# Ada columns loaded one pair ahead and pinned on VectorE, and spread otherwise over a two-layer decoder trunk

## Chip, cores, metric

The kernel runs on one core of one Trainium2 chip. The time is device microseconds for one execution of the whole program. It is compared as the median of several runs.

## What is computed

A trunk of two layers, 256 tokens of 1024 numbers. Layer 0 mixes tokens with a gated convolution, layer 1 with differential attention; a product-key expert layer ("peer", 16384 experts) follows each mixer. Each of these four sub-layers is modulated by a vector c:

```python
def ada_mod(c, w, b):
    m = silu(c) @ w + b            # w: 1024 x 3072
    shift, scale, gate = split(m, 3)
    return shift, 1.0 + scale, 1.0 + gate
for i in range(2):
    shift, scale, gate = ada_mod(c, ada_w[i, 0], ada_b[i, 0])
    f = (short_conv_mixer if i == 0 else diff_attention)(x * scale + shift, ...)
    x = layer_norm(alpha * x + gate * f, ln_g[i, 0], ln_b[i, 0])
    shift, scale, gate = ada_mod(c, ada_w[i, 1], ada_b[i, 1])
    f = peer_ffn(x * scale + shift, w_q, sub_keys, u, v)   # u, v: 16384 x 1024 each
    x = layer_norm(alpha * x + gate * f, ln_g[i, 1], ln_b[i, 1])
```

## The kernel before

**Matrix products.** TensorE (PE) works in a format with a shortened mantissa, so each fp32 operand is split in a high and a low part and each product is made of three. A weight block of 128x1024 fp32 (512 KB) goes through `load`: SyncE (SP) issues its DMA into a buffer `raw`; ScalarE (ACT) copies the high part (L87); VectorE (DVE) subtracts it for the low part (L90, below "subtraction"). The two parts take two of the ten `spt` buffers, so five blocks can be split at once. `raw` has six buffers; the conv mixer adds twelve of its own and attention four. SP issues in a fixed order, and a DMA waits on SP until the last reader of its buffer is done: for a weight block that is its subtraction.

**Ada products.** One pair is two columns of 128x1024 of `ada_w`: `ada_column` loads a column into a `raw` buffer, and one DVE instruction multiplies it by silu(c) and adds it up (L177, "product"). Four pairs make a unit, which ends in one small addition (L186). Twelve pairs run in the conv mixer, 24 in peer 0 and four in peer 1, from generators called `fill`, one pair at each `advance(fill)`; `drain` runs the rest.

**The peer layer.** `steps()` yields steps which `pipeline(steps, 3)` runs: the first half of a step (loads and splits) is issued three steps ahead of its second half (matmuls). Below a V step is one block of `peer_v`: 12 matmuls of 128x512. Two V steps share one `wh` (ACT copy of the gated activations, L87) and one `wl` (its DVE subtraction, L90), each with two buffers. The order is U steps; U with gates; a stretch with U, V and gates; V with gates; and last a stretch of 40 V steps, called the last V stretch here and numbered from 0. Gates are DVE instructions (L824 to L828, L839) around small matmuls (L837). In the last V stretch X, the layer's input, is also multiplied by `ln_g` and has `ln_b` added: `Norm.affine`, four DVE instructions of 128x1024 (L297), behind two loads into `raw` buffers. The matmul loop is the same for all.

**The conv mixer** ends with y (L375 to L378, DVE), from which the output projection's matmuls (L351) follow.

**What sets the order.** A scheduler orders the instructions of each engine when the kernel is built, unless `keep_in_program_order` pins one behind all that was traced on its engine before it. In the conv mixer SP's DMAs are pinned so (`ordered` isn't empty). How often the fill advances:

```python
                if n % 2 == 1:               # U, V and gates
                    yield advance(fill)
...
                if n % 3 == 2:               # the last V stretch
                    yield advance(fill)
```

Of the kernel before, what the change touches and what calls it, by code (L numbers as in the profile page):

```python
# [11 lines left out]
F32 = mybir.dt.float32  # L12
# [8 lines left out]
P = 128  # L21
T = 256
NT = T // P
# [20 lines left out]
def tile_trunk(ctx: ExitStack, tc: tile.TileContext, x, c, columns, ada_w, ln_g, ln_b, conv_w_in_a, conv_w_in_b,  # L44
# [134 lines left out]
    def ada_unit(i, s, part):  # L179
        a = small.tile([P, KC], F32, tag="ada", name="ada", bufs=2)  # L180
        for q in range(KC // 2):
            for f in [ada_column(i, s, part, n, a[:, n:n + 1]) for n in (2 * q, 2 * q + 1)]:
                f()
            yield
        at = slice(None), 2 * i + s, slice(KC * part, KC * part + KC)
        dve.tensor_tensor(mod[at], a, ada_bT[at], op=ALU.add)  # L186
        yield
# [47 lines left out]
    class Norm:  # L235
# [56 lines left out]
        def affine(self, _):  # L292

            gb = ln_params(self.i, self.s)
            for t in range(NT):
                for n, op in enumerate((ALU.mult, ALU.add)):
                    dve.tensor_tensor(X[:, t, :], X[:, t, :], gb[n], op=op)  # L297
# [158 lines left out]
    def attn_mixer(j, li, hT, ap, prep, late):  # L456
# [145 lines left out]
        def steps():  # L602
# [10 lines left out]
            for h0 in range(0, HEADS, 2):  # L613
# [14 lines left out]
                if h0 == 4:  # L628
                    yield None, late
# [15 lines left out]
    def peer(i, hT, pp, fill, prep, late):  # L645
# [239 lines left out]
        def steps():  # L885
# [29 lines left out]
            for n, (gs, u) in enumerate(zip(gates(1, n2), us(2))):  # L915
                yield next(v01)
                yield u
                yield from gs
                if n % 2 == 1:
                    yield advance(fill)  # L920
# [5 lines left out]
            for n, v in enumerate(vs(2)):  # L926
                yield v
                if n % 3 == 2:
                    yield advance(fill)
                if n == 6:  # L930
                    yield None, late
                if n == n2 - 8:
                    yield drain(fill)
                    yield None, prep
# [5 lines left out]
    def units(*which):  # L940
        for w in which:
            yield from ada_unit(*w)

    with tc.tile_pool(name="cp", bufs=1) as cp, tc.tile_pool(name="cs", bufs=12) as more:
        streams.append(more)
        hT = [ht.tile([P, KC, T], F32R, tag=n, name=n) for n in ("hh", "hl")]
        fill = units((0, 0, 2), (0, 1, 0), (0, 1, 1))
# [5 lines left out]
    fill = units((0, 1, 2), (1, 0, 0), (1, 0, 1), (1, 0, 2), (1, 1, 0), (1, 1, 1))  # L953
    with tc.tile_pool(name="pp", bufs=1) as pp:
        late, norm = norm.affine, Norm(0, 1, (1, 0), ada)
        acc = peer(0, hT, pp, fill, norm.prepare, late)
    hT = norm(acc)
    with tc.tile_pool(name="ap", bufs=1) as ap, tc.tile_pool(name="as", bufs=4) as more:
        streams.append(more)
        late, norm = norm.affine, Norm(1, 0, (1, 1), ada)  # L960
# [3 lines left out]
    with tc.tile_pool(name="pp", bufs=1) as pp:  # L964
        late, norm = norm.affine, Norm(1, 1, None, ada)
        acc = peer(1, hT, pp, units((1, 1, 2)), norm.prepare, late)
# [49 lines left out]
```

## Time and profile before

| | |
|---|---|
| median of 3 runs | 1965.9 us (1965.88 to 1968.01) |
| profiled execution | 1965.55 us |
| its span, first to last instruction | 1963.8 us |
| mean granted TensorE clock | 0.985 |
| busy: PE, DVE, ACT | 1888.5, 1554.3, 899.7 us |
| chain of work that ended last | PE 91%, DVE 4%, DMA 3% |

A profile is of one execution. Its timelines give start and length of each instruction or run of like ones, and in brackets how long the engine was idle before and what released it. Idle time of PE is what counts first here.

### The profile page before, as it was taken

Reading aid. Unit: us, or ns where it says so; the run is one execution under the profiler, and the core shown is the slowest. Engines: PE = TensorE matmul, PEld = TensorE weight load, DVE = VectorE, ACT = ScalarE, POOL = GpSimd, SP = SyncE. Lnnn points to the kernel's source line nnn. Section 1 sums busy time; section 2 is a strip of 40 time slices with the busy share of each in tenths; the row PEclk is TensorE's granted clock in tenths of the full one; section 3 lists DMA queues with packets and bytes.
Section 4 is the critical chain, followed back from the end, with each engine's and each line's share of the span. In section 5 each row is a group of like instructions: output and inputs, shape, how many; then the busy total and the mean of one; then the engine's idle time right before and its main releaser. Section 6 shows DMA issues by size and latency. Waiting matters only on the chain.

```text
span 1963.8 us, 36953 instructions
## 1 busy us (share of the span) xinstructions
PE 1888.5 (96%) x14858; PEld 1722.1 (88%) x14858; DVE 1554.3 (79%) x3150; ACT 899.7 (46%) x1179; POOL 9.5 (0%) x28
## 2 busy tenths in 40 slices
PE   7959999999999999989989899999999999999997
PEld 6949999999999988877789699999999999888786
DVE  7988987887888888876677789878877766788755
ACT  4524555434444444434465545554344444444443
POOL 0000000000000000000100000000000000000000
PEclk9979999999999999989999899999999999999999
DMA  9954556556777765557754245555567555555563
GB/s 384 370 172 151 174 174 188 158 162 211 243 241 257 236 204 172 172 181 265 260 171 138 76 151 177 178 183 161 162 209 225 176 175 173 172 172 176 173 195 100
DMA packets 104412, 378.87 MB, mean 193 GB/s; under 512 B 11568, under 2 KB 12208, under 8 KB 104240
## 3 DMA queue, kind: packets, MB, share of 16 engines
q1 hardware_dynamic: 104096, 376.42, 59.4%
q8 instruction: 116, 1.90, 0.4%
q14 instruction: 56, 0.46, 0.1%
q10 hardware_dynamic: 144, 0.09, 0.0%
HBM read 375.42 MB, written 1.05 MB: 192 GB/s over the span
## 4 chain that ended last, share of the span: by engine, by line
PE 91%; DVE 4%; DMA 3%; issue 1%; ACT 1%; SPq 0%; DVEq 0%; ACTq 0%
PE acc L873 34%; PE ps L141 15%; PE ps L142 15%; PE ps L143 15%; PE ps L837 4%; PE acc L351 2%; PE acc L142 2%; PE acc L141 1%; PE acc L143 1%; DVE spt L90 1%; DVE raw L177 1%; DMA raw<-in_ada_w 1%; DMA raw<-in_conv_w_in_a 1%; DMA X<-in_x 1%; PE ps L516 0%
## 5 line engine op out<-in xcount | busy, mean ns | idle before, releaser
L87 ACT ACTIVATE spt<-raw 128x1024 fp32r<-128x1024 f32 x608 | 640.6, 1057 | 737.7 <-PE ps L142 415.6
L90 DVE TENSOR_TENSOR spt<-raw,spt 128x1024 fp32r<-128x1024 f32 x608 | 739.8, 1220 | 161.9 <-ACT spt L87 157.4
L141 PE MATMUL ps<-hh,spt 128*128 128x256 f32 x2400 | 685.4, 286 | 3.5 <-DVE hh L214 3.5
L142 PE MATMUL ps<-hl,spt 128*128 128x256 f32 x2400 | 681.2, 284 | 0.2
L143 PE MATMUL ps<-hh,spt 128*128 128x256 f32 x2400 | 680.6, 284 | 0.0
L873 PE MATMUL acc<-spt,wh 128*128 128x512 f32 x2048 | 567.0, 396 | 3.5 <-ACT wh L87 3.5
L141 PEld LDWEIGHTS ps<-hh,spt 128*128 128x128 f32 x2400 | 460.8, 192 | 7.3 <-issue 4.2
L142 PEld LDWEIGHTS ps<-hl,spt 128*128 128x128 f32 x2400 | 461.4, 192 | 3.9 <-DVE hl L90 0.7
L143 PEld LDWEIGHTS ps<-hh,spt 128*128 128x128 f32 x2400 | 461.3, 192 | 0.0
L873 PEld LDWEIGHTS acc<-spt,wh 128*128 128x128 f32 x2048 | 376.8, 189 | 75.5 <-ACT wh L87 3.8
L873 PE MATMUL acc<-spt,wl 128*128 128x512 f32 x1024 | 320.1, 392 | 5.6 <-DVE wl L90 5.6
L873 PEld LDWEIGHTS acc<-spt,wl 128*128 128x128 f32 x1024 | 191.9, 188 | 47.2 <-DVE wl L90 7.6
L177 DVE SCALAR_TENSOR_TENSOR raw<-raw,csb 128x1024 f32<-128x1024 f32 x96 | 116.2, 1220 | 55.7 <-DMA raw<-in_ada_w 55.5
L839 DVE SCALAR_TENSOR_TENSOR ring<-ps,ring 128x368 f32<-128x368 f32 (+2 forms) x192 | 98.1, 511 | 70.1 <-PE ps L837 69.4
L87 ACT ACTIVATE wh<-ring 128x512 fp32r<-128x512 f32 x128 | 79.9, 627 | 159.4 <-PE acc L873 149.7
L824 DVE TENSOR_TENSOR A<-iota_e,jT 128x1024 f16<-128x1024 f16 x192 | 130.7, 682 | 0.0
L828 DVE TENSOR_TENSOR B<-B,gT 128x368 f16<-128x368 f16 (+2 forms) x384 | 124.4, 332 | 3.9
L90 DVE TENSOR_TENSOR wl<-ring,wh 128x512 fp32r<-128x512 f32 x128 | 87.9, 688 | 38.8 <-ACT wh L87 38.4
L837 PEld LDWEIGHTS <-A 128*128 128x128 f16 x3072 | 91.0, 96 | 31.2 <-issue 14.7
L837 PE MATMUL ps<-B,A 128*128 128x46 f16 (+2 forms) x3072 | 111.9, 182 | 6.7 <-DVE B L828 6.7
L804 ACT ACTIVATE ring<-ps 128x512 f32<-128x512 f32 x128 | 74.6, 583 | 33.8 <-PE ps L143 33.8
L826 DVE TENSOR_TENSOR B<-iota_e,iT 128x368 f16<-128x368 f16 (+2 forms) x192 | 63.1, 330 | 0.0
(203 smaller groups left out, 1175.9 us busy)
## 6 DMA issues: line engine op xcount, KB each, us to landing
raw<-in_peer_u SPq DMA_DIRECT2D x256, 512.0 KB, 3.9
raw<-in_peer_v SPq DMA_DIRECT2D x256, 512.0 KB, 3.9
raw<-in_ada_w SPq DMA_DIRECT2D x96, 512.0 KB, 4.7
raw<-in_peer_w_q SPq DMA_DIRECT2D x32, 512.0 KB, 3.9
raw<-in_attn_w_qk SPq DMA_DIRECT2D x16, 512.0 KB, 4.3
raw<-in_conv_w_in_a SPq DMA_DIRECT2D x12, 512.0 KB, 10.2
raw<-in_conv_w_in_b SPq DMA_DIRECT2D x12, 512.0 KB, 10.2
raw<-in_conv_w_out SPq DMA_DIRECT2D x8, 512.0 KB, 6.9
```

What stands on the lines that cost most here:

```text
L87: act.activation(o, i, AF.Copy, scale=scale)
L90: return eng.tensor_tensor(o, a, b, op=ALU.subtract)
L141: pe.matmul(ps, ah, bh, start=first, stop=False)
L142: pe.matmul(ps, ah, bl, start=False, stop=False)
L143: pe.matmul(ps, al, bh, start=False, stop=last)
L177: return lambda: dve.scalar_tensor_tensor(w, w, 1.0, csb, op0=ALU.mult, op1=ALU.mult, accum_out=dst)
L804: act.activation(ring[:, s:s + 2, :].rearrange("p j t -> p (j t)"), st["ps"], AF.Gelu)
L824: dve.tensor_tensor(by_two(A), numbers(0, KEYS), pairs(jT, KEYS), op=ALU.is_equal)
L828: dve.tensor_tensor(by_two(B[:, h]), by_two(B[:, 1]), pairs(gT[:, h], n), op=ALU.mult)
L837: pe.matmul(ps[:, t, :], A[:, t, :], B[:, h, t, :], start=h == 0, stop=h == 1)
L839: dve.scalar_tensor_tensor(r, ps.rearrange("p t j -> p j t"), 1.0 / GSCALE, r, op0=ALU.mult, op1=ALU.mult)
L873: pe.matmul(acc[t][hf], lhs[:, jj, rows], rhs[:, hf * 512:(hf + 1) * 512], start=first and jp == 0 and jj == 0, stop=last and last_pair an ...
```

## The change

The generator of ada products now loads a pair's two columns one advance before it multiplies them, and outside the conv mixer pins the products where they are traced on DVE. The affine becomes a step with a first half (the two loads, so three steps ahead) and a second (the four DVE instructions, pinned). The fill advances on every third step instead of every second in the stretch with U, V and gates, and on every second instead of every third in the last V stretch, up to step 29. So peer 0 makes 13 of its 24 pairs ahead of the last V stretch's own advances instead of 16, and 11 instead of 8 there.

```diff
-    def ada_unit(i, s, part):
-        a = small.tile([P, KC], F32, tag="ada", name="ada", bufs=2)
-        for q in range(KC // 2):
-            for f in [ada_column(i, s, part, n, a[:, n:n + 1]) for n in (2 * q, 2 * q + 1)]:
-                f()
-            yield
-        at = slice(None), 2 * i + s, slice(KC * part, KC * part + KC)
-        dve.tensor_tensor(mod[at], a, ada_bT[at], op=ALU.add)
-        yield
+    def ada_units(*which):
+
+        def compute(at, a, fs, final):
+            for f in fs:
+                ins = f()
+                if not ordered:
+                    tc.keep_in_program_order(ins)
+            if final:
+                dve.tensor_tensor(mod[at], a, ada_bT[at], op=ALU.add)
+
+        loaded = None
+        for i, s, part in which:
+            a = small.tile([P, KC], F32, tag="ada", name="ada", bufs=3)
+            at = slice(None), 2 * i + s, slice(KC * part, KC * part + KC)
+            for q in range(KC // 2):
+                fs = [ada_column(i, s, part, n, a[:, n:n + 1]) for n in (2 * q, 2 * q + 1)]
+                if loaded:
+                    compute(*loaded)
+                    yield
+                loaded = at, a, fs, q == KC // 2 - 1
+        compute(*loaded)
         yield
...
-        def affine(self, _):
-
-            gb = ln_params(self.i, self.s)
-            for t in range(NT):
-                for n, op in enumerate((ALU.mult, ALU.add)):
-                    dve.tensor_tensor(X[:, t, :], X[:, t, :], gb[n], op=op)
+        def affine(self):
+
+            def first():
+                return ln_params(self.i, self.s)
+
+            def second(gb):
+                for t in range(NT):
+                    for n, op in enumerate((ALU.mult, ALU.add)):
+                        tc.keep_in_program_order(dve.tensor_tensor(X[:, t, :], X[:, t, :], gb[n], op=op))
+
+            return first, second
...
-                if n % 2 == 1:
+                if n % 3 == 2:
                     yield advance(fill)
...
-                if n % 3 == 2:
+                if n % 2 == 1 and n < n2 - 10:
                     yield advance(fill)
                 if n == 6:
-                    yield None, late
+                    yield late
```

The first place is the last V stretch of peer 0 on DVE. Each `wl` waits for PE to have done with the pair of steps two before it, so it tells how far DVE is ahead of PE. Before, around one pair of columns there (the first `wl` is that of steps 12 and 13, the second that of 14 and 15):

```order
1101 L90 TENSOR_TENSOR wl<-ring,wh 128x512 [waits PE_49,Activation_49]
1102 L90 TENSOR_TENSOR spt<-raw,spt 128x1024 [waits DMAHW3_49,Activation_49]
1103 L90 TENSOR_TENSOR spt<-raw,spt 128x1024 [waits DMAHW6_49,PE_49,Activation_49]
1104 L90 TENSOR_TENSOR wl<-ring,wh 128x512 [waits PE_49,Activation_49]
1105 L90 TENSOR_TENSOR spt<-raw,spt 128x1024 [waits DMAHW7_49,Activation_49]
1106 L177 SCALAR_TENSOR_TENSOR raw,ada<-raw,csb 128x1024 [waits DMAHW4_49,DVE_49]
1107 L90 TENSOR_TENSOR spt<-raw,spt 128x1024 [waits DMAHW0_49,PE_49,Activation_49]
1108 L177 SCALAR_TENSOR_TENSOR raw,ada<-raw,csb 128x1024 [waits DMAHW5_49,DVE_49]
1109 L90 TENSOR_TENSOR wl<-ring,wh 128x512 [waits PE_49,Activation_49]
```

And now, from the `wl` of steps 12 and 13 on; five such rows, here called a period, stand there seven times in all:

```order
1100 L90 TENSOR_TENSOR wl<-ring,wh 128x512 [waits PE_49,Activation_49]
1101 L90 TENSOR_TENSOR spt<-raw,spt 128x1024 [waits DMAHW6_49,Activation_49]
1102 L90 TENSOR_TENSOR spt<-raw,spt 128x1024 [waits DMAHW7_49,Activation_49]
1103 L177 SCALAR_TENSOR_TENSOR raw,ada<-raw,csb 128x1024 [waits DMAHW4_49]
1104 L177 SCALAR_TENSOR_TENSOR raw,ada<-raw,csb 128x1024 [waits DMAHW5_49]
1105 L90 TENSOR_TENSOR wl<-ring,wh 128x512 [waits PE_49,Activation_49]
1106 L90 TENSOR_TENSOR spt<-raw,spt 128x1024 [waits DMAHW2_49,Activation_49]
1107 L90 TENSOR_TENSOR spt<-raw,spt 128x1024 [waits DMAHW3_49,Activation_49]
1108 L177 SCALAR_TENSOR_TENSOR raw,ada<-raw,csb 128x1024 [waits DMAHW0_49,DVE_49]
1109 L177 SCALAR_TENSOR_TENSOR raw,ada<-raw,csb 128x1024 [waits DMAHW1_49,DVE_49]
```

What moved: before, DVE subtracted blocks 16 and 17 behind the `wl` of steps 14 and 15; now it subtracts blocks 11 and 12 behind the `wl` of steps 12 and 13. So against the same `wl` it does blocks of three steps less. The wait for PE at every second subtraction (its `spt` buffer, just coming free) is gone, and both products of a pair stand behind both subtractions.

On SP, in the same stretch, before:

```order
137 L69 DMA raw<-in_ada_w 128x1024 x2
138 L69 DMA raw<-in_peer_v 128x1024 x3
139 L69 DMA raw<-in_ada_w 128x1024 x2
140 L69 DMA raw<-in_peer_v 128x1024 x3
141 L69 DMA raw<-in_ada_w 128x1024 x2
142 L69 DMA raw<-in_peer_v 128x1024 x3
143 L69 DMA raw<-in_ada_w 128x1024 x2
```

And now:

```order
138 L69 DMA raw<-in_ada_w 128x1024 x2
139 L69 DMA raw<-in_peer_v 128x1024 x2
140 L69 DMA raw<-in_ada_w 128x1024 x2
141 L69 DMA raw<-in_peer_v 128x1024 x2
142 L69 DMA raw<-in_ada_w 128x1024 x2
143 L69 DMA raw<-in_peer_v 128x1024 x2
144 L69 DMA raw<-in_ada_w 128x1024 x2
145 L69 DMA raw<-in_peer_v 128x1024 x2
146 L69 DMA raw<-in_ada_w 128x1024 x2
```

What moved: two loads of ada columns now stand behind every two loads of V, not every three or six. The two V loads of a period take the two `raw` buffers of the two V blocks just ahead of them, from here to the end of the fill; the other four buffers hold two pairs of columns.

The second place is the way into that stretch on DVE, with the last gates and X's affine, before:

```order
1070 L828 TENSOR_TENSOR B<-B,gT 128x320 [waits DVE_49]
1071 L90 TENSOR_TENSOR spt<-raw,spt 128x1024 [waits DMAHW0_49,PE_49,Activation_49]
1072 L828 TENSOR_TENSOR B<-B,gT 128x320 [waits DVE_49] x2
1073 L177 SCALAR_TENSOR_TENSOR raw,ada<-raw,csb 128x1024 [waits DMAHW7_49]
1074 L828 TENSOR_TENSOR B<-B,gT 128x320 [waits DVE_49]
1075 L839 SCALAR_TENSOR_TENSOR ring<-ps,ring 128x40x8 [waits PE_49]
1076 L177 SCALAR_TENSOR_TENSOR raw,ada<-raw,csb 128x1024 [waits DMAHW0_49]
1077 L839 SCALAR_TENSOR_TENSOR ring<-ps,ring 128x40x8 [waits PE_49]
1078 L90 TENSOR_TENSOR wl<-ring,wh 128x512 [waits Activation_49] x2
1079 L297 TENSOR_TENSOR X<-X,raw 128x1024 [waits DMAHW3_49]
1080 L297 TENSOR_TENSOR X<-X,raw 128x1024
1081 L90 TENSOR_TENSOR spt<-raw,spt 128x1024 [waits DMAHW1_49,PE_49,Activation_49]
```

And now, from the `wl` of steps 8 and 9 on (ahead of it stand, in this order, the `wl` of the first two pairs of steps, the subtraction of block 5, `wl`, the subtraction of 6, two products, `wl`, the subtraction of 7 and two products):

```order
1088 L90 TENSOR_TENSOR wl<-ring,wh 128x512 [waits PE_49,Activation_49]
1089 L187 TENSOR_TENSOR mod<-ada,smT 128x8 [waits DVE_49]
1090 L90 TENSOR_TENSOR spt<-raw,spt 128x1024 [waits DMAHW1_49,Activation_49]
1091 L90 TENSOR_TENSOR spt<-raw,spt 128x1024 [waits DMAHW2_49,Activation_49]
1092 L313 TENSOR_TENSOR X<-X,raw 128x1024 [waits DMAHW4_49]
1093 L90 TENSOR_TENSOR wl<-ring,wh 128x512 [waits PE_49,Activation_49]
1094 L313 TENSOR_TENSOR X<-X,raw 128x1024 [waits DMAHW5_49,DVE_49]
1095 L313 TENSOR_TENSOR X<-X,raw 128x1024
1096 L90 TENSOR_TENSOR spt<-raw,spt 128x1024 [waits DMAHW3_49,Activation_49]
1097 L177 SCALAR_TENSOR_TENSOR raw,ada<-raw,csb 128x1024 [waits DMAHW7_49]
1098 L177 SCALAR_TENSOR_TENSOR raw,ada<-raw,csb 128x1024 [waits DMAHW0_49]
1099 L313 TENSOR_TENSOR X<-X,raw 128x1024 [waits DVE_49]
```

What moved: before, a product stood among the last gates' B's and another between the two L839, each of a column loaded just before. Now both stand together ahead of the last three B's, and the two products that stood one gate group earlier have gone. Behind the gates, three pairs of products stand among the subtractions of blocks 6 to 10, and X's affine (L313 now), which stood ahead of block 5, stands behind block 9.

## Rows read from the trace of the kernel before

**Rows 1.** The page: groups (busy, mean ns, idle before), then a DMA median to landing.
```profile
L87 ACT ACTIVATE spt<-raw 128x1024 fp32r<-128x1024 f32 x608 | 640.6, 1057 | 737.7 <-PE ps L142 415.6
L90 DVE TENSOR_TENSOR spt<-raw,spt 128x1024 fp32r<-128x1024 f32 x608 | 739.8, 1220 | 161.9 <-ACT spt L87 157.4
...
L177 DVE SCALAR_TENSOR_TENSOR raw<-raw,csb 128x1024 f32<-128x1024 f32 x96 | 116.2, 1220 | 55.7 <-DMA raw<-in_ada_w 55.5
...
raw<-in_peer_v SPq DMA_DIRECT2D x256, 512.0 KB, 3.9
```

**Rows 2.** Busy time by stretch, columns in its first line.
```profile
core 0: us, PE busy (x) PEld busy (x) DVE busy (x) ACT busy (x) POOL busy (x), PEclk, DMA share, GB/s
...
100.00:120.00 20.00, 8.05 (x35) 6.22 (x33) 20.00 (x39) 1.25 (x2) 0.00 (x0) 0.77 0.79 261
480.00:700.00 220.00, 220.00 (x1790) 200.71 (x1787) 184.73 (x306) 96.50 (x111) 0.00 (x0) 1.00 0.75 245
840.00:866.00 26.00, 19.59 (x167) 15.71 (x166) 20.77 (x39) 8.91 (x11) 0.00 (x0) 0.85 0.66 214
866.00:886.00 20.00, 20.00 (x76) 16.08 (x76) 10.19 (x11) 7.74 (x10) 0.00 (x0) 0.85 0.53 158
```

**Rows 3.** Timeline of PE, end of peer 0; idle and releaser in brackets.
```profile
858.80 0.22 PE L837 MATMUL ps<-B,A 128*128 128x40 f16 x1 [2.78 <-DVE B L828]
860.17 0.21 PE L837 MATMUL ps<-B,A 128*128 128x40 f16 x1 [1.16 <-DVE B L828]
...
865.81 3.78 PE L873 MATMUL acc<-spt,wh 128*128 128x512 f32 x8 [2.20 <-ACT wh L87]
```

**Rows 4.** Waits: engine, line, released by: us in total, times, longest.
```profile
DVE raw L177 <- DMA raw<-in_ada_w: 55.5, 31, 4.3
...
PE acc L873 <- DVE wl L90: 5.6, 4, 1.9
```

**Rows 5.** Timeline of DVE over the same stretch.
```profile
853.67 1.23 DVE L177 SCALAR_TENSOR_TENSOR raw<-raw,csb 128x1024 f32<-128x1024 f32 x1 [1.06 <-DMA raw<-in_ada_w]
...
861.43 1.23 DVE L177 SCALAR_TENSOR_TENSOR raw<-raw,csb 128x1024 f32<-128x1024 f32 x1 [1.08 <-DMA raw<-in_ada_w]
...
885.63 1.23 DVE L177 SCALAR_TENSOR_TENSOR raw<-raw,csb 128x1024 f32<-128x1024 f32 x1 [3.83 <-DMA raw<-in_ada_w]
...
886.78 0.69 DVE L90 TENSOR_TENSOR wl<-ring,wh 128x512 fp32r<-128x512 f32 x1
```

**Rows 6.** Chain of waits, 840 to 990 us: start, length, what.
```profile
839.92 2.72 PE acc L873 x12
...
859.91 3.47 DMA raw<-in_ada_w
...
873.06 4.67 DMA raw<-in_peer_v
...
880.70 4.84 DMA raw<-in_ada_w
```

**Rows 7.** Timeline of ACT in the last V stretch.
```profile
915.90 0.63 ACT L87 ACTIVATE wh<-ring 128x512 fp32r<-128x512 f32 x1 [1.66 <-PE acc L873]
...
918.62 1.06 ACT L87 ACTIVATE spt<-raw 128x1024 fp32r<-128x1024 f32 x1 [1.14 <-PE acc L873]
```

**Rows 8.** Timeline of DVE, end of the conv mixer.
```profile
85.78 1.23 DVE L90 TENSOR_TENSOR spt<-raw,spt 128x1024 fp32r<-128x1024 f32 x1 [0.81 <-ACT spt L87]
...
89.57 1.23 DVE L90 TENSOR_TENSOR spt<-raw,spt 128x1024 fp32r<-128x1024 f32 x1 [1.69 <-ACT spt L87]
...
119.36 0.75 DVE L378 TENSOR_TENSOR y<-y,g 128x256 f32<-128x256 f32 x2
```

**Rows 9.** Timeline of PE, same place.
```profile
120.28 3.78 PE L351 MATMUL acc<-spt,yh 128*128 128x512 f32 x8 [12.23 <-ACT yh L87]
```

**Rows 10.** Timeline of PE, peer 1, entry to the last V stretch.
```profile
1842.78 2.10 PE L873 MATMUL acc<-spt,wh 128*128 128x512 f32 x8 [1.32 <-ACT wh L87]
1845.96 1.19 PE L873 MATMUL acc<-spt,wl 128*128 128x512 f32 x4 [1.08 <-DVE wl L90]
```

More of the change, by code (lines that the diff above doesn't have):

```diff
@@ L927, in steps @@
                 yield v
-                if n % 3 == 2:
+                if n % 2 == 1 and n < n2 - 10:
                     yield advance(fill)
                 if n == 6:
-                    yield None, late
+                    yield late
                 if n == n2 - 8:
@@ L937, in peer @@
         return acc
-    def units(*which):
-        for w in which:
-            yield from ada_unit(*w)
     with tc.tile_pool(name="cp", bufs=1) as cp, tc.tile_pool(name="cs", bufs=12) as more:
@@ L946, in tile_trunk @@
         hT = [ht.tile([P, KC, T], F32R, tag=n, name=n) for n in ("hh", "hl")]
-        fill = units((0, 0, 2), (0, 1, 0), (0, 1, 1))
+        fill = ada_units((0, 0, 2), (0, 1, 0), (0, 1, 1))
         norm = Norm(0, 0, (0, 1), cp)
@@ L952, in tile_trunk @@
     ordered.clear()
-    fill = units((0, 1, 2), (1, 0, 0), (1, 0, 1), (1, 0, 2), (1, 1, 0), (1, 1, 1))
+    fill = ada_units((0, 1, 2), (1, 0, 0), (1, 0, 1), (1, 0, 2), (1, 1, 0), (1, 1, 1))
     with tc.tile_pool(name="pp", bufs=1) as pp:
-        late, norm = norm.affine, Norm(0, 1, (1, 0), ada)
+        late, norm = norm.affine(), Norm(0, 1, (1, 0), ada)
         acc = peer(0, hT, pp, fill, norm.prepare, late)
@@ L959, in tile_trunk @@
         streams.append(more)
-        late, norm = norm.affine, Norm(1, 0, (1, 1), ada)
+        late, norm = norm.affine(), Norm(1, 0, (1, 1), ada)
         acc = attn_mixer(0, 1, hT, ap, norm.prepare, late)
@@ L964, in tile_trunk @@
     with tc.tile_pool(name="pp", bufs=1) as pp:
-        late, norm = norm.affine, Norm(1, 1, None, ada)
-        acc = peer(1, hT, pp, units((1, 1, 2)), norm.prepare, late)
+        late, norm = norm.affine(), Norm(1, 1, None, ada)
+        acc = peer(1, hT, pp, ada_units((1, 1, 2)), norm.prepare, late)
     norm(acc)
```

## Prediction

> **What bounds the kernel now.** First the page's table: PE is busy 1888.5 of 1963.8 us, so about 75 us of PE idle time are all that a change of VectorE and DMA order can touch, and much of it belongs to the start and the norms. Then the busy time by stretch [rows 2]: in the long stretch with U, V and gates (480 to 700 us) PE is busy 220.00 of 220 us although pairs of products run there; nothing is to be had there. At the end of the conv mixer it is the reverse: DVE is busy 20.00 of 20 us, PE 8.05. In the last stretches of peer 0 both have gaps. Then the waits [rows 4]: DVE waits 55.5 us for columns of `ada_w`, in 31 places. That is much, but idle time of DVE; PE waits for a `wl` in four places, 5.6 us in all. So the time the change aims at is mostly time in which PE worked on. What PE does wait for in its last V stretch shows on its timeline [rows 3] and in the chain [rows 6]: a few us. On ACT, a high part is copied there as soon as PE frees a buffer ("1.14 <-PE acc") [rows 7]: before, weights are as far ahead as the five pairs of `spt` buffers allow. That lead is what hides DVE's waits.
>
> **Peer 0's last V stretch, the main term.** A V step takes PE 2.72 us [rows 6], two take 5.44. DVE's work for two steps is now one `wl`, two subtractions and two products. On the timeline the product at 885.63 and the `wl` at 886.78 start 1.15 apart, and the next instruction 0.60 behind the `wl` [rows 5]; a subtraction is as long as a product (mean 1220 ns both) [rows 1]. So 0.60 + 4 x 1.15 = 5.2 us of 5.44: it fits, barely.
>
> What doesn't fit is the way through the two `raw` buffers left for V. The load of block k+2 is issued when block k's subtraction ends. It lands, ACT copies 1.06 us [rows 1], DVE subtracts (1.2 us with its start), and the hand-overs take some 0.05 each. So a buffer goes round once in the landing time plus 2.3 us, and PE wants it each 5.44: the landing would have to take 3.1 us or less. No row has that. The shortest load on the chain took 3.47, the median of V is 3.9, a V load behind another 4.67, and the first column of a pair 4.84 [rows 1, 6]. The first load of a period is issued 2.2 us behind the last column, the second 1.2 us behind the first. I take 4.1 us for the first (just over the median) and 4.7 for one right behind another (the 4.67 row). So a period takes 4.1 + 2.3 = 6.4 us, 1.0 longer than PE's.
>
> Now block by block, in us from PE's start of step 0 (step k would end at 2.72 (k+1)); five blocks are ready at 0, as before. Block 5 is subtracted by 5.0, as PE frees its buffer at 2.7. Then `wl` waits for the end of step 1 and block 6 is done at 8.4; products to 10.7. Block 7's load was issued at 9.5, behind the affine's two: landed 14.2, copied 15.3, done 16.4; in time (wanted at 19.0), but it holds DVE up, and two products follow to 18.7. Block 8's buffer came free with the first of them at 17.55: landed 22.25, done 24.5, wanted at 21.8: **PE waits 2.7.** Block 9 is done at 25.7; three of the affine's instructions and a `wl` follow to 29.7. Block 10, issued at 24.5: done 30.9, wanted 29.9: **1.0.** Products, the affine's last and `wl` to 34.9. Block 11, issued at 30.9: landed 35.0, done 37.3, wanted 33.6: **3.7.** From here the periods run as above, and blocks 13, 15, 17, 19, 21 and 23 are late by 1.0 each: **6.0.** Sum 13.4 us. Against it stand the waits for `wl` of before, which the new order replaces: 5.6 less the 1.08 that is peer 1's [rows 4, 10], 4.5. Term: **+8.9.** With 3.5 us for every landing the same walk gives about 6 (block 8 0.3, block 10 0.4, block 11 3.1, the rest 0.4 each), so +1.5; with 4.84 for all about 19 (2.9, 1.7, 4.4, and 1.7 each), so +14.5. Those are its bounds.
>
> The page "DMA: Bandwidth & Descriptors" of the Trainium skill (Anatomy of one DMA, the GpSimd path) gives a fixed 2.0 us plus bytes over 436 GB/s. By it, as an estimate, a block of 512 KB would land in 3.2 us and the period would be 5.5 us, so that the steady part would cost next to nothing. The trace disagrees: 3.47 is the shortest here, for a load that had nothing right ahead of it, and the median is 3.9 [rows 1, 6].
>
> **The last gates of peer 0.** PE idles 2.78 + 1.16 + 2.20 us between 856 and 865.8 [rows 3], since B's stand behind products, and products behind columns just loaded (1.06 and 1.08 us of waits on DVE) [rows 5]. Without the earlier pair (two products and the 1.06: 3.4 us) the first of the last B's is ready at 857.1. A subtraction and two products, which need not wait any more, follow to 860.5, three B's to 861.2, the gate matmuls to 861.9; ring and `wh` (0.4 and 0.63 [rows 7]) and hand-overs bring step 0 to 863.2. The other rings also wait on PE, whose clock is at half there (below), so I take 863.9 and not 865.81: **-1.9** (bounds -0.9 and -2.6).
>
> **Conv mixer.** The matmuls at 120.28 waited 12.23 us for y [rows 9], whose last instruction ends DVE's queue there [rows 8]. All 24 products of the mixer still stand ahead of it. Four go from behind the last z to before it, but DVE had idled only 0.81 + 1.69 us in the 35 us before [rows 8]. Loads a pair ahead fill some of that: **-1.0** (0 to -2.5). The two more columns on SP ahead of the conv weights push them back by about 2.6, hidden by weights that are copied only when PE frees buffers.
>
> **Peer 1.** The affine stood ahead of the first `wl`; now it stands behind block 9. PE's wait of 1.08 goes; the 1.32 before it hangs on ring and `wh`, which don't move [rows 10]: **-1.1** (0 to -1.1). Its four pairs of columns lie in the stretch where PE never idles, as do the 13 of peer 0: **0**. The three pairs that leave that stretch free DVE, not PE [rows 2]. In attention the affine's two loads start much earlier and its four instructions move later, behind other scores; PE's waits there are for ACT. I take 0, with 1.5 either way.
>
> **Sum.** 8.9 - 1.9 - 1.0 - 1.1 = +4.9. The profiled execution took 1965.55, 0.35 below the median, and its span 1963.8 plus 1.75 around it, which stay. So the profile would read about 1970.4 and the median 1970.8 us.
>
> **The rivals.** *The clock falls as well.* The stalls at 856 to 865.8 were followed by matmuls at 1.2 GHz: eight took 3.78 us, where the same eight in peer 1 took 2.10, and the two windows around read 0.85 [rows 2, 3, 10]. Two windows of 26 and 20 us at 0.85 hold 30% of 46, or 13.8 us, at half clock, which is 6.9 us of PE's work lost, part of it in waits. If the stall of 3.7 us at block 11 and those near it do the same, that is about 5 us more: 1976. Against it: at half clock PE also wants blocks later, so most is paid once.
>
> *Landings at the short bound.* The columns are issued far ahead of their products, so V loads may meet an empty queue; then the V stretch costs +1.5 to +3 and the gains eat it: about 1965. This is also what the skill's rule would come to.
>
> *Faster: DVE's waits were what mattered.* The 55.5 us of DVE's waits go, and with them every wait of PE for `wl`; V keeps its lead because the scheduler's order holds DVE less than I think. It decides at a landing of 3.1 us or at V loads spread over more buffers. Then -4.5 -1.9 -1.0 -1.1 = -8.5: 1957.4. For it speaks that before, waits of 3.83 us for a column hardly reached PE [rows 5]; against it, that no load lands in 3.1.
>
> *Faster at the conv mixer.* If y really comes up by what left the stretch behind z (four products and two subtractions, 6 x 1.15 = 6.9 us), the sum is 8.9 - 1.9 - 6.9 - 1.1 = -1.0: 1964.9; with the short landings too, 1958 to 1959. It would need DVE to have had room before z, of which the rows show 2.5 us.
>
> **How the numbers follow.** My forecast 0.46; clock 0.12; short landings 0.20; DVE's waits 0.16; conv 0.06. The prediction is the forecast's 1970.8. Its own range, with gains and losses at their bounds and not all at once, is 1964 to 1978. The range goes down to 1959.5, which leaves out most of the faster case, and up to 1981, which takes in the clock. A measurement tells about 0.2%, 3.9 us, from no change. Faster by that (below 1962): the DVE case, half the conv case and a little of the short one, 0.23. Same: most of the short case, a quarter of the forecast, half the conv case, 0.29. Slower: 0.48.
>
> **What would show it.** In the changed profile: DVE's waits for `ada_w` near zero in peer 0 (31 places before); ACT copies in the last V stretch released by DMA of V and no longer by PE; `PE acc L891` (L873 now moved) waiting on DVE subtractions of weights at steps 8, 10, 11 and then every second step; the stretch from step 0 to the end of the fill longer by 8 to 9 us; step 0 some 2 us earlier; the conv gap 11 us instead of 12.23; no `wl` wait of 1.08 in peer 1. The prediction is wrong if PE's V steps run without gaps although DVE's waits are gone, or if V's landings there are 3.1 us or less, or if the stretch with U, V and gates gains gaps.

## The result and the profile after

| | before | after |
|---|---|---|
| median of 4 runs | 1966.4 us | 1986.5 us (1984.5 to 1986.6) |
| ratio | | 1.0098 [1.0083, 1.0113] |
| profiled span | 1963.8 us | 1984.7 us |
| mean granted TensorE clock | 0.985 | 0.981 |

The kernel is slower by 20 us. The direction was forecast (+4.9 us), the size was not: 1986 lies outside the range of 1959.5 to 1981. From the page of the changed kernel (matmul L873 is now L891, gates L837 and L839 now L855 and L857, conv L351 now L369, the affine L297 now L313; in attention the bias L520 now L538, the scalings L537 and L538 now L555 and L556):

```profile
PE 1899.9 (96%) x14858; PEld 1725.9 (87%) x14858; DVE 1556.5 (78%) x3150; ACT 900.1 (45%) x1179; POOL 9.5 (0%) x28
...
L891 PE MATMUL acc<-spt,wh 128*128 128x512 f32 x2048 | 571.0, 398 | 13.8 <-ACT spt L87 10.5
...
L177 DVE SCALAR_TENSOR_TENSOR raw<-raw,csb 128x1024 f32<-128x1024 f32 x96 | 114.2, 1222 | 1.2 <-DMA raw<-in_ada_w 1.1
```

The edit does what its words say: DVE's 55.5 us of waits for columns [rows 4] are 1.1. In their place PE's V matmuls wait for ACT's copies of weights. PE is also "busy" 11.4 us longer with the same matmuls: the mean clock is lower, and some waits lie inside runs of matmuls, which count as busy (below).

To see where the 20.9 us of span lie, each trace is cut at the first transpose of X behind each norm ("norm") and at the first V matmul behind the last gates ("step 0"). Read from PE's timelines, in us from the span's start: norms before at 134.76, 987.84 and 1115.17, after at 133.07, 996.30 and 1135.41; step 0 before at 865.81 and 1842.78 [rows 3, 10], after at 863.50 and 1864.94.

| stretch, us | before | after | difference | forecast |
|---|---|---|---|---|
| start to the conv norm | 134.8 | 133.1 | -1.7 | -1.0 |
| peer 0, norm to step 0 | 731.0 | 730.4 | -0.6 | -1.9 |
| peer 0, last V stretch, to its norm | 122.0 | 132.8 | **+10.8** | +8.9 |
| attention, norm to norm | 127.3 | 139.1 | **+11.8** | 0 |
| peer 1, norm to step 0 | 727.6 | 729.5 | +1.9 | 0 |
| peer 1, step 0 to the end | 121.0 | 119.8 | -1.3 | -1.1 |

**The last V stretch.** PE's timeline there, only the rows with a gap (in brackets the idle time and its releaser):

```profile
888.70 1.99 PE L891 MATMUL acc<-spt,wh 128*128 128x512 f32 x6 [1.61 <-ACT spt L87]
...
896.04 1.99 PE L891 MATMUL acc<-spt,wh 128*128 128x512 f32 x6 [1.25 <-ACT spt L87]
...
902.50 1.99 PE L891 MATMUL acc<-spt,wh 128*128 128x512 f32 x6 [3.08 <-ACT spt L87]
...
916.86 1.99 PE L891 MATMUL acc<-spt,wh 128*128 128x512 f32 x6 [0.90 <-ACT spt L87]
...
930.73 1.99 PE L891 MATMUL acc<-spt,wh 128*128 128x512 f32 x6 [1.36 <-ACT spt L87]
...
938.14 1.99 PE L891 MATMUL acc<-spt,wh 128*128 128x512 f32 x6 [1.33 <-ACT spt L87]
```

With 923.26 (0.33) and 944.82 (0.59) these are all that wait for ACT: 10.45 us. One more, 0.18 us at 952.00, waits for DVE. Counted in steps of 12 matmuls from step 0 at 863.50 they stand before steps 8, 10, 11, 15, 17, 19, 21 and 23. Each is followed by a second, smaller wait that PE's own rows hide, since it lies inside a run of six matmuls. The weight loads' timeline (PEld) shows it:

```profile
930.72 0.76 PEld L891 LDWEIGHTS acc<-spt,wh 128*128 128x128 f32 x4 [1.78 <-ACT spt L87]
931.98 0.30 PEld L891 LDWEIGHTS acc<-spt,wh 128*128 128x128 f32 x2 [0.50 <-DVE spt L90]
```

Four matmuls need only the block's high part, the fifth needs the low part, which DVE's subtraction delivers 1.2 us behind the copy: 0.5 us more for each late block, and 0.44 at step 13 without a gap ahead of it. Six matmuls behind a gap take 1.99 us, six others 1.52. The chain of work says what each late block hangs on:

```profile
901.39 1.06 ACT spt L87
902.45 0.02 issue
902.48 1.24 DVE spt L90
903.71 0.02 issue
903.73 5.00 DMA raw<-in_peer_v
908.73 0.02 issue
908.75 1.07 ACT spt L87
909.83 0.02 issue
909.85 1.24 DVE spt L90
911.09 0.02 issue
911.10 4.62 DMA raw<-in_peer_v
```

This is the loop through two `raw` buffers: load, copy, subtraction, and the next load at once; no PE in it. One round is 7.37 us here (903.73 to 911.10). From one late block's subtraction to the next on DVE's timeline it is the same 7.37 (902.48 to 909.85), then 6.99, 6.42, 7.45 and 7.41, where PE needs a block each 5.44. On ACT a part of the copies is now released by the DMA and no longer by PE (before, 240.4 us in 164 places by PE, and no row for V's loads), in the list of waits:

```profile
ACT spt L87 <- PE acc L891: 199.3, 139, 3.2
...
ACT spt L87 <- DMA raw<-in_peer_v: 68.7, 34, 5.7
```

This row by itself is no loss: it reads 67.8 and 102.3 in the two kernels below that are faster than the one before. What counts is that PE's gaps stand behind it.

**Attention.** DVE's timeline before, where the affine's four instructions stand, 37.6 us behind the norm at 987.84:

```profile
1025.46 2.35 DVE L297 TENSOR_TENSOR X<-X,raw 128x1024 f32<-128x1024 f32 x2
1027.73 1.22 DVE L90 TENSOR_TENSOR spt<-raw,spt 128x1024 fp32r<-128x1024 f32 x1
1028.87 2.35 DVE L297 TENSOR_TENSOR X<-X,raw 128x1024 f32<-128x1024 f32 x2
```

and after, 85 us behind the norm at 996.30, between the bias additions (L538), maxima (L540) and scalings (L555, L556) of the third of four groups of heads:

```profile
1080.93 0.68 DVE L540 TENSOR_REDUCE mx<-s 128x4 f32<-128x512 f32 x1
1081.52 1.22 DVE L313 TENSOR_TENSOR X<-X,raw 128x1024 f32<-128x1024 f32 x1
1082.65 0.69 DVE L538 TENSOR_TENSOR s<-ps,bias 128x512 f32<-128x512 f32 x1
1083.25 2.36 DVE L313 TENSOR_TENSOR X<-X,raw 128x1024 f32<-128x1024 f32 x2
1085.52 0.18 DVE L550 RECIPROCAL mx<-mx 128x4 f32<-128x4 f32 x1
1085.61 0.67 DVE L538 TENSOR_TENSOR s<-ps,bias 128x512 f32<-128x512 f32 x1
1086.18 2.36 DVE L90 TENSOR_TENSOR spt<-raw,spt 128x1024 fp32r<-128x1024 f32 x2
1088.45 1.23 DVE L313 TENSOR_TENSOR X<-X,raw 128x1024 f32<-128x1024 f32 x1
```

No row has a bracket: DVE has no idle time, so 4.6 us of affine push all that is behind them. PE is released late by the scaling, and the last group's scores (L534) start late; on PE's timeline, down to the first of the output products behind the last group (L369):

```profile
1093.91 0.59 PE L558 MATMUL ps<-ident,s 128*128 128x128 f32 x2 [3.33 <-DVE s L556]
...
1099.45 3.16 PE L534 MATMUL ps<-k,q 64*128 64x128 f32 x16
1102.54 1.20 PE L369 MATMUL acc<-spt,yh 128*128 128x512 f32 x4
...
1122.12 1.52 PE L369 MATMUL acc<-spt,yh 128*128 128x512 f32 x4 [0.47 <-ACT yh L87]
...
1126.57 0.38 PE L589 MATMUL ps<-ident,o 128*128 128x128 f32 x2
```

The same matmuls before:

```profile
1084.82 2.37 PE L516 MATMUL ps<-k,q 64*128 64x128 f32 x16
1087.12 1.20 PE L351 MATMUL acc<-spt,yh 128*128 128x512 f32 x4
...
1103.34 1.20 PE L351 MATMUL acc<-spt,yh 128*128 128x512 f32 x4 [0.47 <-ACT yh L87]
...
1106.23 0.38 PE L571 MATMUL ps<-ident,o 128*128 128x128 f32 x2
```

The last group's 16 score matmuls started 96.98 us behind the norm before, and the next matmuls 2.30 us later; now they start 103.15 us behind it, and the next 3.09 us later. So 6.2 of the 11.8 us are lost when the last group begins, 5.6 behind that. The busy time by stretch shows both, and the last V stretch:

```profile
core 0: us, PE busy (x) PEld busy (x) DVE busy (x) ACT busy (x) POOL busy (x), PEclk, DMA share, GB/s
...
480.00:700.00 220.00, 220.00 (x1785) 201.00 (x1784) 179.68 (x293) 95.51 (x109) 0.00 (x0) 1.00 0.72 231
...
886.00:906.00 20.00, 13.87 (x52) 9.46 (x51) 14.69 (x16) 6.33 (x7) 0.00 (x0) 0.96 0.71 227
...
926.00:946.00 20.00, 16.59 (x67) 11.82 (x65) 15.69 (x21) 7.19 (x8) 0.00 (x0) 1.00 0.88 294
1084.00:1096.00 12.00, 8.19 (x41) 6.27 (x40) 11.93 (x22) 6.14 (x14) 0.00 (x0) 0.98 0.43 131
1096.00:1106.00 10.00, 9.24 (x43) 7.38 (x42) 5.66 (x25) 3.39 (x17) 0.00 (x0) 0.68 0.00 0
1123.00:1135.00 12.00, 7.01 (x24) 5.06 (x22) 8.28 (x19) 5.15 (x10) 0.00 (x0) 0.78 0.01 1
```

In 1084 to 1096 DVE is busy 11.93 of 12 us and PE 8.19. Right behind PE's wait the granted clock is 0.68, part of it at 1.2 GHz, and it is 0.78 again in the last 12 us, where the same place before read 0.97. The stretch with U, V and gates (480 to 700) runs without a gap, as forecast.

### The profile page after: what moved, and what is told of

It is laid out like the page before. It is cut to its first block, busy times and chain, and to the rows that moved or that the text cites. A ratio compares the mean times of both kernels' runs of the same rounds, so it can differ in the third digit from the quotient of the medians.

```text
span 1984.7 us, 36911 instructions
## 1 busy us (share of the span) xinstructions
PE 1899.9 (96%) x14858; PEld 1725.9 (87%) x14858; DVE 1556.5 (78%) x3150; ACT 900.1 (45%) x1179; POOL 9.5 (0%) x28
## 4 chain that ended last, share of the span: by engine, by line
PE 88%; DVE 5%; DMA 4%; ACT 2%; issue 1%; SPq 0%; DVEq 0%; ACTq 0%
PE acc L891 32%; PE ps L141 15%; PE ps L142 15%; PE ps L143 15%; PE ps L855 4%; DMA raw<-in_peer_v 2%; DVE spt L90 2%; PE acc L142 2%; PE acc L141 1%; PE acc L143 1%; PE acc L369 1%; DVE raw L177 1%; ACT spt L87 1%; DMA raw<-in_conv_w_in_a 1%; DMA X<-in_x 0%
## 5 line engine op out<-in xcount | busy, mean ns | idle before, releaser
L891 PE MATMUL acc<-spt,wh 128*128 128x512 f32 x2048 | 571.0, 398 | 13.8 <-ACT spt L87 10.5
L891 PEld LDWEIGHTS acc<-spt,wh 128*128 128x128 f32 x2048 | 375.8, 189 | 92.0 <-ACT spt L87 13.8
L891 PE MATMUL acc<-spt,wl 128*128 128x512 f32 x1024 | 319.5, 392 | 0.0
L891 PEld LDWEIGHTS acc<-spt,wl 128*128 128x128 f32 x1024 | 192.2, 188 | 40.0
L857 DVE SCALAR_TENSOR_TENSOR ring<-ps,ring 128x368 f32<-128x368 f32 (+2 forms) x192 | 98.4, 513 | 94.2 <-PE ps L855 93.6
L855 PE MATMUL ps<-B,A 128*128 128x46 f16 (+2 forms) x3072 | 112.1, 182 | 7.2 <-DVE B L846 7.2
L855 PEld LDWEIGHTS <-A 128*128 128x128 f16 x3072 | 91.3, 96 | 31.7 <-issue 14.1
## 6 DMA issues: line engine op xcount, KB each, us to landing
raw<-in_conv_w_in_a SPq DMA_DIRECT2D x12, 512.0 KB, 10.2
raw<-in_conv_w_in_b SPq DMA_DIRECT2D x12, 512.0 KB, 10.2
```

Source lines behind the costliest of these rows:

```text
L855: pe.matmul(ps[:, t, :], A[:, t, :], B[:, h, t, :], start=h == 0, stop=h == 1)
L857: dve.scalar_tensor_tensor(r, ps.rearrange("p t j -> p j t"), 1.0 / GSCALE, r, op0=ALU.mult, op1=ALU.mult)
L891: pe.matmul(acc[t][hf], lhs[:, jj, rows], rhs[:, hf * 512:(hf + 1) * 512], start=first and jp == 0 and jj == 0, stop=last and last_pair an ...
```

## The experiments

Two places lose, so there are two questions: what in the V stretch costs, and what in attention. First each place is put back by itself, then both. Where more than one run is told, the ratio is to the kernel before on the same chip; a single run is compared by its stretches.

### Attention's affine as before

```diff
                 if h0 == 4:
-                    yield late
+                    yield None, late
...
-        late, norm = norm.affine(), Norm(1, 0, (1, 1), ada)
+        late, norm = norm.affine_before, Norm(1, 0, (1, 1), ada)
```

`affine_before` is the old method. 

> The changed kernel, with the affine of the attention stretch alone put back: loads and four unpinned DVE instructions at one place. Between the two norms around attention the changed kernel takes 139.1 us, the kernel before 127.3. Theory A (the four affine instructions, pinned in the middle of the softmax, stand in the chain from scores to values): the stretch falls to 127 to 129 us and the whole to 1975 us. Theory B (the two early loads hold raw buffers and delay weights): the same here, so the next run has to tell. Theory C (the order of attention moved for another reason): the stretch stays at 137 us or more, the whole at 1985 us.

Measured: 1973.5 us, 1.003 [1.0019, 1.0042]. Attention takes 129.1 us instead of 139.1; the V stretch does not gain (134.1). So 10.0 of the 11.8 us in attention belong to the affine there.

### The old spacing, loads still ahead and products pinned

```diff
-                if n % 3 == 2:
+                if n % 2 == 1:
                     yield advance(fill)
...
-                if n % 2 == 1 and n < n2 - 10:
+                if n % 3 == 2:
                     yield advance(fill)
```

> The changed kernel with the fill advanced as often as before in both stretches of peer 0 (every second step beside U, every third in the last V stretch), still loaded a pair ahead and pinned. Theory A for the last V stretch (two loads of columns for every two of V leave V two raw buffers, so a block goes round in 6.4 us against 5.44): with three or more buffers for V the waits of PE for high parts go from 10.5 to under 5 us, the time from step 0 to the norm falls from 132.8 to 123 to 126 us, the whole to 1977 to 1980 us if attention stays as it is. Rival (the pinned products themselves hold the subtractions up, however many there are): the stretch stays at 130 us or more, the whole at 1984 us or more.

Measured: 1974.8 us, 1.0038 [1.0027, 1.0049]. The V stretch takes 123.4 us with four pairs behind step 0, instead of 132.8 with ten (counted by the products on DVE's timeline), and peer 0 up to step 0 takes 726.8, 4.3 less than before; the next kernel, whose peer 0 is the same, takes 728.9. Attention stays at 139.2.

### Both put back

The two diffs above together. 

> Both put back at once: the fill advances as often as before in peer 0, and the affine of attention is as before; columns are still loaded a pair ahead and pinned, and the affine is a pinned step in both peers. If the two losses are apart (the last V stretch +10.8, attention +11.8) and the rest of the change is a gain, the pieces measured so far add: step 0 of peer 0 at 860.2 (865.8 before), V stretch 123.4 (122.0), attention 127 to 129 (127.3), peer 1 to its step 0 727.7 (727.6), the end 119.8 (121.0): some 3 to 6 us less than before, 1960 to 1964 us. Rival: the attention order is a matter of luck with the time at which the stretch begins; then attention stays at 135 or more and the whole is at 1970 us or more.

Measured: 1961.1 us, 0.9969 [0.9956, 0.9981]: faster than before. V stretch 121.5, attention 129.1. So what is left of the change gains about 0.3%: by stretches 1.7 us up to the conv norm, 2.1 up to step 0 of peer 0 and 1.4 at the end of peer 1. The new spacing and the affine's new place in attention lose more than that.

### The spacing alone, on the kernel before

The second diff reversed, on the kernel before: columns loaded and multiplied in one advance, nothing pinned. 

> The kernel before with only the new spacing of the fill in peer 0 (every third step beside U, every second in the last V stretch); columns loaded where they are multiplied, nothing pinned. Theory A (V's round through two buffers makes the loss): the columns hold their buffers shorter, but each pair makes DVE wait 3 us or more for a fresh column, once for every two V steps, with V subtractions behind it; so the stretch from step 0 to the norm takes longer than the 122.0 of before and about as long as the changed kernel's 132.8: 128 to 138 us, the whole 1972 to 1982. Rival (the spacing itself costs nothing, loading ahead does): 122 to 125 us, the whole 1966 to 1969.

Measured: one run of 1976.2 us; V stretch 131.4, +9.3 over before. That is nearly the whole loss, without the two-buffer loop. The list of waits of this kernel (its V matmul is L873, as before):

```profile
DVE raw L177 <- DMA raw<-in_ada_w: 45.7, 33, 3.2
...
PEld acc L873 <- DVE wl L90: 15.6, 10, 2.6
...
PE acc L873 <- DVE wl L90: 11.2, 8, 2.2
```

Here DVE waits for columns just loaded, and PE for `wl` behind them: 11.2 us in eight places, seven of them with 10.2 us in this stretch, where the changed kernel lost 10.5 to ACT's copies. The first of the seven (1.8) hangs in the chain on the affine's loads, the others stand behind products. The way of the loss differs, its size hardly. Eleven pairs stand behind step 0 here, where the kernel before has six: what costs is how many pairs lie in this stretch.

### Half columns

```diff
-        sync.dma_start(w, ada_w[i, s, part, n])
-        return lambda: dve.scalar_tensor_tensor(w, w, 1.0, csb, op0=ALU.mult, op1=ALU.mult, accum_out=dst)
+        h = slice(0, D if ordered else D // 2)
+        sync.dma_start(w[:, h], ada_w[i, s, part, n][:, h])
+        return lambda: dve.scalar_tensor_tensor(w[:, h], w[:, h], 1.0, csb[:, h], op0=ALU.mult, op1=ALU.mult, accum_out=dst)
```

> The changed kernel, leaving out half of every ada column outside the conv mixer: the loads and products take 128x512 instead of 128x1024, in the same order and the same buffers. It halves the columns' work for DMA and DVE and leaves V its two raw buffers. Theory A (the way round two buffers: landing 4.1 us plus copy, subtraction and hand-overs): V's landings get a little shorter, to about 3.7 us, so a period stays at 6.0 us against 5.44; the time from step 0 to the norm falls from 132.8 only to 127 to 130 us. Rival (DVE, busy 5.2 of each 5.44 us, or the DMA engines, at 0.88, are full): with 2.3 us of DVE and 2.6 us of DMA less in each period PE's waits go, and the stretch falls to 122 to 124 us.

Measured: one run of 1979.9 us; V stretch 126.5 instead of 132.8, which lies between what the two theories gave. The chain of this kernel between 893 and 935 has V loads of 3.6 to 4.0 us and one of 4.72 (ahead of them one of 5.72), where the changed kernel's has 4.1 to 5.4: with less in front of them on the queue, V loads land some 0.6 us sooner on the mean. But half-size columns also shorten DVE's products (0.61 us from start to start instead of 1.14, so 1.1 us for a pair and not the 2.3 that the expectation took), so this run doesn't part the two.

### Every pair beside U

```diff
                 yield from gs
-                if n % 2 == 1:
+                if n % 5 in (1, 2, 4):
                     yield advance(fill)
```

on the kernel with both put back; all 24 pairs of peer 0 are then done before step 0. 

> The faster version so far (fill spaced as before, attention's affine as before, the rest as changed: 1961.1 us) with the spacing moved the other way: three advances in five steps beside U, V and gates instead of one in two, so that all 24 pairs of peer 0 lie there and none in the last V stretch. Theory A (columns cost where V has only a few raw buffers and DVE is short of time, and nothing where PE is full): the last V stretch falls from 121.5 to 115 to 118 us, the way from the conv norm to step 0 stays at 727 to 730, the whole is 1955 to 1958 us. Rival (DVE, busy 185 of 220 us beside U, can't take 8 more pairs): the way to step 0 grows by 3 us or more and the whole is at 1961 us or more.

Measured: 1955.5 us, 0.9949 [0.9936, 0.9963], the fastest here. The V stretch takes 112.95 us; peer 0 up to step 0 takes 728.8, where it took 728.9 with both put back. Busy time by stretch:

```profile
480.00:700.00 220.00, 220.00 (x1781) 200.00 (x1781) 199.93 (x336) 95.65 (x109) 0.00 (x0) 1.00 0.84 279
...
882.00:902.00 20.00, 20.00 (x90) 16.57 (x89) 13.65 (x14) 9.95 (x12) 0.00 (x0) 1.00 0.79 246
902.00:922.00 20.00, 20.00 (x90) 16.53 (x89) 11.89 (x11) 8.99 (x11) 0.00 (x0) 1.00 0.61 190
```

Beside U, DVE is busy 199.93 of 220 us (179.68 in the changed kernel, 193.01 with both put back) and PE still has no gap; in the V stretch PE is now busy 20.00 of 20. Over these kernels the V stretch takes 112.95 us with no pair in it, 121.5 and 123.4 with four, 122.0 with six (the kernel before), and 131.4 to 134.1 with ten or eleven. Some of that is clock: the first 16 matmuls of the stretch take 3.80 us here and took 6.64 before. The next kernel has ten pairs in the stretch and starts it as fast as this one (8 matmuls in 2.14 us); it takes 131.4, so 1.85 us for each pair. Over all these kernels, less the slower start, a pair costs some 1 to 2 us.

### Attention: loaded early, not pinned

`second` as in the change, without `keep_in_program_order`, for attention's affine alone. 

> The changed kernel, with the affine of the attention stretch still loaded three steps ahead, but its four instructions not pinned. Theory A (the pinned place costs): the stretch between the norms falls from 139.1 to 127 to 130 us, the whole to 1975 to 1977 us. Theory B (the early loads cost): it stays at 137 us or more, the whole at 1984 to 1987 us. Theory C: as theory B.

Measured: 1985.1 us, 1.0096 [1.0079, 1.0113]; attention 140.5. Nothing comes back: the pin alone is not the cause.

### Attention: early and pinned, but no place in the lead

A step with a first half counts among the three that `pipeline` keeps ahead; here the affine's doesn't.

```diff
-                    waiting += 1
+                    waiting += not isinstance(step, Aside)
...
-                    yield late
+                    yield Aside(late)
```

> The changed kernel, with the affine of attention as it is (two loads ahead, four pinned instructions), but as a step that takes none of the three places by which loads and softmax run ahead. Theory D (the affine, now a step with a first half, takes one of the three places, so the softmax of the third group of heads is issued one step later and comes short of time before its values): attention falls from 139.1 to 127 to 130 us, the whole to 1975 us. Rival E (loads that start early or instructions that are pinned move the order of scores by themselves): attention stays at 135 us or more.

Measured: one run of 1986.0 us; attention 138.8. The place in the lead is not what costs. But the four instructions have moved too: they stand 62 to 67 us behind the norm (below).

### Attention: loaded in place, pinned

```diff
-                    yield late
+                    yield None, lambda _: late[1](late[0]())
```

> The changed kernel, with the affine of attention loaded where it is used, as before, but its four instructions pinned. Theory D (the place in the lead): no place is taken, so attention falls to 127 to 131 us. Theory F (the four instructions, 4.6 us of DVE behind the scores of the third group, whatever loads them): attention stays at 135 us or more. In the order of the built kernel the third group's scores stand earlier than in the changed kernel but later than before, so a value between, 131 to 135, would say that the pinned place makes a part.

Measured: one run of 1985.6 us; attention 139.0. With the loads where they were, the pin is enough for the whole loss.

### Attention: the loads alone, and the instructions alone

```diff
-                    yield late
+                    yield late[0], seen
```

`seen` reads one column of each load (128x1). 

> The changed kernel, leaving out the affine's four instructions in attention (X is neither multiplied nor added to there); its two loads stay three steps ahead, and one-element-wide instructions read the buffers. Theory F (the four instructions stand between the scores and the values of the last groups of heads on DVE, wherever they are put but in the first group's slack): attention falls from 139.1 to 126 to 130 us, the whole to 1974 us. Theory B (two early loads of other data hold buffers or move the order of the projections): it stays at 135 us or more.

Measured: one run of 1975.7 us; attention 128.3. The other half of the pair:

```diff
-                    yield late
+                    yield None, lambda _: late[1]((csb, csb))
```

> The changed kernel, leaving out the loads of the affine in attention: its four pinned instructions take another tile that is there anyway (so the numbers differ), at the same place in program order. Theory F: attention stays at 137 us or more, since the 4.6 us stand behind the third group's scores as before. Theory B: it falls to 130 us or less, since nothing is loaded.

Measured: one run of 1987.3 us; attention 141.3. The four instructions at that place cost all of it, the early loads nothing. With the loads alone, the third group's scores start as far behind the norm as in the changed kernel (81.3 and 86.3 us), but the last group's at 98.0 instead of 103.15. Without the instructions DVE has room there again and PE works on:

```profile
1084.00:1096.00 12.00, 10.78 (x65) 8.89 (x64) 10.74 (x23) 7.93 (x23) 0.00 (x0) 1.00 0.30 87
```

against 11.93 on DVE and 8.19 on PE in the changed kernel.

### Attention: aside and not pinned

The two edits of the second and third attention kernels together. 

> The changed kernel, with the affine of attention loaded three steps ahead without a place in the lead, and not pinned. Two runs put these instructions early and unpinned or pinned without a place, and both stayed at 139 to 140 us. If the place in the lead was what kept the unpinned one slow, attention falls to 127 to 130 us here. If it is that the loads are there early, so that the four instructions are put ahead of the first group's softmax and move the order behind them, it stays at 137 us or more.

Measured: one run of 1982.5 us; attention 136.7. Still slow, though neither pinned nor in the lead. In the two unpinned kernels the four instructions stand 31 to 37 us behind the norm, ahead of where they stood before, and in the one with early loads, pinned and without a place in the lead, 62 to 67. In none of these three is DVE full around PE's wait (8.62, 7.43 and 7.42 of 10 us). What they share is that PE comes to the last of the third group's scores only 89.5 to 93.7 us behind the norm (85.8 before, 86.3 in the changed kernel) and then waits 3.9 to 4.8 us for their scaling. So a full DVE explains the changed kernel, the one loaded in place (busy 11.47 of 12 us) and the one with the instructions alone (12.00), and not these three. Why the scheduler's order has the scores so late in them stays open.

## Why the prediction was wrong

**Attention, the step that failed.** It said of the affine's instructions that they "move later, behind other scores; PE's waits there are for ACT. I take 0, with 1.5 either way." The runs show +11.8: 6.2 until the last group's scores, and 5.6 behind. Of the 5.6, the rows shown give 0.8 to a slower clock at the scores (3.09 us against 2.30) and 1.6 at the first output products behind the last group (1122.12 to 1126.57, 4.45 us, against 2.89): the granted clock reads 0.52 from 1097.4 to 1102.5 and 0.63 from 1122 to 1126.6, against 1.00 at both places before. The other 3.2 lie in between, around the last group's values, where PE now waits 0.51 us for ACT and 1.64 for DVE. The other stretches had been walked instruction by instruction, this one was judged by the engine that PE waits for now. ACT's exponentials wait for DVE's maxima in turn, and how full DVE would be at the new place was left out of the working. With attention's affine put back the time is 1973.5 us, inside the range, so the loss that no term foresaw is what carried it out.

**The last V stretch: the mechanism held, the size was near.** Stalls were forecast before steps 8, 10, 11 and every second one to 23; they stand before just these, that of 13 only as 0.44 us of a low part. Forecast 2.7, 1.0, 3.7 and six of 1.0, in all 13.4; measured, gap and low part together, 2.1, 1.75, 3.6, 0.4, and 1.4, 0.85, 1.9, 1.8 and about 1.1: 14.9. What ends PE's wait is ACT's copy, and then DVE's subtraction, not the subtraction alone as the prediction had it. Less the 4.5 us that went, that makes 10.4 of the measured 10.8. The rest is small because clock terms that the forecast left out nearly cancel: steps 11 and 12 lost some 1.6 us behind the stall of 3.08, and the first 16 matmuls of the stretch, slow in both kernels, took 5.29 us instead of 6.64. The landing term was too small: 4.1 us for the first load of a period was forecast, rounds of 6.4; in the chain they take 4.1 to 5.4, rounds of 6.4 to 7.45.

**The bigger half of that answer was missed.** The prediction priced the loop and not the count. The spacing alone costs 9.3 us on the kernel before, so the loop isn't what makes the pairs dear there: with columns just loaded they are about as dear, by waits for `wl`. Of the stretch with U, V and gates the prediction said that "nothing is to be had there". That was true for taking pairs out of it, and it hid that more could be put in for nothing.

**The last gates** were to give 1.9 and gave 0.6. On PE's timeline the gaps ahead of step 0 are 1.27, 3.47 and 1.30, in all 6.04 us, where they were 6.14 [rows 3] and 0.28 more at 862.95: one pair's two products (2.3 us, 856.53 to 858.82 on DVE) still stand ahead of the last B's, and step 0's 863.50 is early mostly by what the conv mixer gave. With the old spacing no pair stands there; gaps of 3.65 and 1.30 are left, and the stretch takes 726.8 and 728.9 us in the two kernels that have it, where the changed kernel takes 730.4.

**The conv mixer** gave 1.7 where 1.0 was taken: the gap of 12.23 [rows 9] is 8.55 and one of 1.66 ahead of it. **Peer 1's** end gave 1.3 (forecast 1.1). Its first part lost 1.9, forecast 0; it is 727.6 to 727.8 us in the kernels with the affine of attention as before or unpinned, 728.9 to 729.7 in all others. Why was not followed further.

**The rivals.** "Landings at the short bound" falls: no V load of that stretch's chain takes less than 4.09 us. By the rule of the Trainium skill's page "DMA: Bandwidth & Descriptors" (Anatomy of one DMA) it would be 3.2, as an estimate. The page gives that rule for DMAs that GpSimd issues, and SyncE issues these, so the runs show only that it does not carry over to them. "DVE's waits were what mattered" falls in its place, but its time (1957.4) was nearly reached by other means: 1961.1 with both losses put back, and 1955.5 with every pair beside U. "The clock falls as well" held where it wasn't looked for. In the V stretch the clock reads 0.96 around the stall of 3.08, and steps 11 and 12 take 4.35 and 3.20 us (902.50 to 910.05), together some 1.6 more than another late step and the one behind it, where the rival had about 5. In attention the rows add up to 3.3: the 0.8 and 1.6 above, and 0.9 at the third group's values (1097.44 to 1099.45, 2.01 us, against 1.09).

## What to carry to other kernels

The price of filler work is that of the stretch it is put in, not that of its instructions: a pair costs 1 to 2 us beside V, whether DVE waits for its columns or the V loads wait for their buffers, and nothing beside U, where PE never runs out. So place filler by PE's slack in each stretch first, and only then care how early it is loaded. When a shared helper is pinned or moved, walk every place that uses it: an instruction that had slots between waits may land in a queue that is full for 12 us, and a stall there is paid again in clock. Or it may move the order of others, as in the unpinned kernels here.

## What the runs showed of the hardware

A late weight block costs PE twice, once for the high part (0.3 to 3.1 us) and about 0.5 us more for the low part, which the weight loads' rows show as a wait and PE's rows only as a longer run. A 512 KB load of V landed in 4.1 to 5.4 us with full columns near it on the queue, mostly in 3.6 to 4.0 with half ones. The granted clock read 0.68 in the 10 us behind a PE wait of 3.33 us in attention (0.52 from 1097.4 to 1102.5).
